# Expert gates of both halves built once in the up stage, the second half's kept in DRAM, and all low parts of the up stage made by GpSimd

## Chip, cores and metric

One core of a Trainium2 chip. The metric is the device time of one launch in microseconds (us), the median of several runs. The profile is one further execution, whose own time stands in the table below.

## The reference, cut to what matters

The program is a transformer block followed by two more layers, for 256 tokens of width 1024 in float32. The part that is changed belongs to the first block's product-key expert layer:

```python
v1, i1 = lax.top_k(s1, 16)                    # per token and head, over 128 keys
v2, i2 = lax.top_k(s2, 16)
cand = (v1[..., :, None] + v2[..., None, :])  # 16 x 16 sums
...
sv, pos = lax.top_k(cand, 16)
eidx = jnp.take_along_axis(i1 * 128 + i2, pos)   # expert number, shortened
gw = softmax(sv)
act = x . u_tab[eidx];  hact = gelu(act) * gw;  y = sum(hact * v_tab[eidx])
```

Each token uses 8 heads x 16 = 128 of 16,384 experts. Expert number = 128 * i1 + i2.

## The kernel before, in words

The kernel does not gather experts. It multiplies all 16,384 rows of `peer_u` with all tokens (the **up stage**), applies gelu, multiplies the result with a dense matrix of gates that is zero for every expert that a token did not choose, and multiplies that with all rows of `peer_v` (the **down stage**). A block is the 128 experts that share one i1. Block b of the activations is a 128 x 256 tile (i2 by tokens), and the 128 blocks lie in two SBUF tensors, `A[0]` for blocks 0 to 63 and `A[1]` for 64 to 127.

Float32 accuracy comes from splitting: every 128 x 1024 weight tile (`wraw`) is copied by ScalarE to a rounded high part (`whi`) and the rest is subtracted into a low part (`wlo`); three matmuls replace one (`mm3`, lines 224 to 229, and `down`, lines 295 to 318). `wraw`, `whi` and `wlo` have three buffers each.

*Up stage* (`u_blocks`, `u_split`, lines 1015 to 1032). For each block: load `peer_u` on SyncE's queue (L249), high part on ScalarE (L1018), low part on GpSimd or VectorE by the set `POOL_U` (L1019), 24 matmuls (L227 to L229), gelu on ScalarE (L1031). Beside it run, by a hand-set ratio of steps per block (`even`): `topk`, blocks 0 to 75, on VectorE; `gates(0)`, blocks 76 to 127; and `ada0`, which loads a 128 x 1024 tile of `ada_w` and reduces it on VectorE (L180), 24 times. While `topk` runs its scratch tiles lie in `A[1]`, which its blocks have not reached.

`gates(half)` (lines 992 to 1009), 32 iterations of 8 tokens: one-hot matrices of i2 (`oa`, L1000) and, for the 64 values of i1 of this half, of i1 (`ob`, L1002) by comparing with `iota`; `ob` times the gate weight (L1003); 8 float32 matmuls give the gates of 8 tokens (L1006; the trace has two instructions for each); VectorE multiplies them into `A[half]` (L1008). The picked indices and weights `iT` lie in SBUF.

*Down stage* (`v_blocks`, lines 1043 to 1052). For each block: load `peer_v` (L249), high part on ScalarE (L1039), low part on VectorE (L1040), the activations split into `wwh` (ScalarE, L217) and `wwl` (VectorE, L222), 12 matmuls of 512 columns (L308, L309, L312). Beside blocks 0 to 63 run `gates(1)` and 40 steps of `ada1` (L180 again), beside blocks 64 to 127 another 32 steps of `ada1`.

Each engine runs its own instructions in order. That order is laid down when the kernel is built, by a scheduler that works on simulated times; program order decides only among what is ready there. So a gate matmul can stand ahead of blocks that come earlier in the program.

Of the kernel before, what the change touches and what calls it, by code (L numbers as in the profile page):

```python
# [18 lines left out]
T = 256  # L19
# [65 lines left out]
def program(tc, I, out, C, taps=None, upto=99):  # L85
# [821 lines left out]
    for c in range(16):  # L907
# [8 lines left out]
        for tt in range(2):  # L916
# [2 lines left out]
    tap("sc", sc)  # L919

    wk = keep.tile([128, 2 * D], F32, name="C8")
    iT = wk[:, 0:768].rearrange("p (j t) -> p j t", j=3)
    iota = wk[:, 768:896]
    oas = itertools.cycle([wk[:, 896:1920].rearrange("p (t i) -> p t i", t=8),
                           wrk.tile([128, 8, 128], F32, name="oa", bufs=1)])
    G.dma_start(iota, C["iota"])

    def topk():
        sels = [flat(b, 1).rearrange("p (s c) -> p s c", s=2) for b in (99, 103)]
        gw = flat(101, 1).rearrange("p (t h k) -> p t h k", t=2, h=8)  # L930
        for tt in range(2):
            rg = flat(88 + 4 * tt, 4)
            v = rg[:, 0:256].rearrange("p (c k) -> p c k", c=16)
            ix = rg[:, 256:512].bitcast(U32).rearrange("p (c k) -> p c k", c=16)
            sv = rg[:, 512:640].rearrange("p (h k) -> p h k", h=8)
            px = rg[:, 640:768].bitcast(U32).rearrange("p (h k) -> p h k", h=8)
            s2 = flat(96, 1)[:, 0:128]
            cand = flat(97, 1)
            for h in range(8):
                for half in range(2):  # L940
                    c = 2 * h + half
                    s1 = sc[:, tt, c]
                    V.max(v[:, c, 0:8], s1)
                    V.max_index(ix[:, c, 0:8], v[:, c, 0:8], s1)
                    V.match_replace(s2, v[:, c, 0:8], s1, -3e38)
                    V.max(v[:, c, 8:16], s2)
                    V.max_index(ix[:, c, 8:16], v[:, c, 8:16], s2)
                yield
                V.tensor_tensor(cand.rearrange("p (a b) -> p a b", a=16),
                                v[:, 2 * h].unsqueeze(2).to_broadcast([128, 16, 16]),  # L950
                                v[:, 2 * h + 1].unsqueeze(1).to_broadcast([128, 16, 16]), op=OP.add)
                V.max(sv[:, h, 0:8], cand)
                V.max_index(px[:, h, 0:8], sv[:, h, 0:8], cand)
                V.match_replace(cand, sv[:, h, 0:8], cand, -3e38)
                V.max(sv[:, h, 8:16], cand)
                V.max_index(px[:, h, 8:16], sv[:, h, 8:16], cand)
                yield

            fx = rg[:, 768:1024].rearrange("p (c k) -> p c k", c=16)
            V.tensor_copy(fx, ix)  # L960
            ab = flat(98, 1).rearrange("p (s h k) -> p s h k", s=2, h=8)
# [19 lines left out]
        V.tensor_reduce(r8, gw, axis=AX.X, op=OP.add)  # L981
        V.reciprocal(r8, r8)
        V.tensor_tensor(gw, gw, r8.unsqueeze(3).to_broadcast([128, 2, 8, 16]), op=OP.mult)
        for tt in range(2):
            pt = ps_tr((128, 384))
            for j, src in enumerate((sels[tt][:, 0], sels[tt][:, 1], gw[:, tt].rearrange("p h k -> p (h k)"))):
                P.transpose(pt[:, j * 128:j * 128 + 128], src, ident)
            ts = slice(tt * 128, tt * 128 + 128)
            V.tensor_copy(iT[:, :, ts], pt.rearrange("p (j t) -> p j t", j=3))
            yield  # L990

    def gates(half):


        io = iota.unsqueeze(1).to_broadcast([128, 8, 128])
        ioh = iota[:, half * 64:half * 64 + 64].unsqueeze(1).to_broadcast([128, 8, 64])
        for t0 in range(0, T, 8):
            ts = slice(t0, t0 + 8)
            oa = next(oas)
            V.tensor_tensor(oa, io, iT[:, 1, ts].unsqueeze(2).to_broadcast([128, 8, 128]), op=OP.is_equal)  # L1000
            ob = wrk.tile([128, 8, 64], F32, name="ob")
            V.tensor_tensor(ob, ioh, iT[:, 0, ts].unsqueeze(2).to_broadcast([128, 8, 64]), op=OP.is_equal)  # L1002
            V.tensor_tensor(ob, ob, iT[:, 2, ts].unsqueeze(2).to_broadcast([128, 8, 64]), op=OP.mult)  # L1003
            pg = ps_tr((128, 8, 64))
            for t in range(8):
                P.matmul(pg[:, t], oa[:, t], ob[:, t], start=True, stop=True)  # L1006
            dst = A[half][:, :, ts]
            V.tensor_tensor(dst, dst, pg.rearrange("p t b -> p b t"), op=OP.mult)  # L1008
            yield

    Ut, Vt = I["peer_u"], I["peer_v"][0]
    POOL_U = set(b for b in range(3, 76) if b % 5) | set(b for b in range(76, 128) if b % 3)
    POOL_V = ()

    def u_split(b):
        raw = unit(Ut[b])
# [19 lines left out]
    def v_split(b):  # L1036
        raw = unit(Vt[b * 128:(b + 1) * 128])
        hi, lo = hilo()
        last_hi[0] = S.activation(hi, raw, AF.Copy)  # L1039
        (G if b in POOL_V else V).tensor_tensor(lo, raw, hi.bitcast(F32), op=OP.subtract)  # L1040
        return hi, lo

    def v_blocks(b0, b1_):
        for b in range(b0, b1_):
            vs = vt.pop(b)
            if b < 126:
                vt[b + 2] = v_split(b + 2)
            wh = wrk.tile([128, T], F32R, name="wwh", bufs=2)
            wl = wrk.tile([128, T], F32R, name="wwl", bufs=2)
# [31 lines left out]
        even(ada0, i, ADA, 100)  # L1081
    for _ in tk:
        pass
    tap("iT", iT)
    g0 = gates(0)
    for i, _ in enumerate(u_blocks(76, 128)):
        even(g0, i, 32, 50)
        even(ada0, i + 76, ADA, 100)
# [628 lines left out]
```

## Time and profile before

| | us |
|---|---|
| median of 3 runs (2226.71 to 2234.04) | 2227.6 |
| the profiled execution, its own time | 2230.72 |
| its span, first to last instruction | 2228.9 |
| TensorE busy, of the span | 2124.5 (95%) |
| VectorE busy | 1697.8 (76%) |
| ScalarE busy | 1011.9 (45%) |
| GpSimd busy | 714.6 (32%) |

A busy time is the sum of an engine's instructions. Matmuls are pipelined, so a TensorE that is busy throughout is not one at its peak; the distance from one matmul's start to the next tells more. In the rows of busy time by stretch the engines stand in the order TensorE matmul (PE), TensorE weight load (PEld), VectorE (DVE), ScalarE (ACT), GpSimd (POOL), each with its count of instructions; the granted TensorE clock, the DMA share and GB/s follow. The up stage runs from about 520 us to 998 us of the span, the first half of the down stage to 1240 us, the second to 1430 us.

### The profile page before, as it was taken

The page shows a single profiled execution, that of the slowest core. Times are in us where ns is not written, and L with a number is a line of the kernel's source. Part 1 is how long each engine was busy: PE and PEld are TensorE (multiplying, and loading weights), DVE is VectorE, ACT ScalarE, POOL GpSimd, SP SyncE. Part 2 cuts the span into 40 slices and gives each one's busy share as a digit, 9 for nine tenths or more (in the row PEclk, how much of TensorE's full clock was granted, in tenths as well). Part 3 has the DMA queues.
Part 4 walks back from the last instruction along what each step waited for, and adds up shares of the span by engine and source line. Part 5 has one row for each costly group of instructions (what it writes and reads, how often), then busy time and mean ns, then how long its engine had stood idle before and what let it go on. Part 6 is the DMA issues. An engine that isn't in the chain of part 4 may idle for free.

```text
span 2228.9 us, 38314 instructions
## 1 busy us (share of the span) xinstructions
PE 2124.5 (95%) x15238; PEld 1966.2 (88%) x15238; DVE 1697.8 (76%) x2671; ACT 1011.9 (45%) x1666; POOL 714.6 (32%) x359
## 2 busy tenths in 40 slices
PE   9999999998788999999999999999989899999999
PEld 8989999998788999998888777899877899888998
DVE  6677688779998456679999787635696778677876
ACT  5645565444343433333443455534533454544554
POOL 2212332203555654430000000132261456344554
PEclk9999999999898999999999999999999999999999
DMA  6544544465454764447667888765331655554552
GB/s 211 162 125 136 166 125 123 152 200 180 166 185 142 227 197 144 130 137 267 234 225 238 295 280 284 195 132 79 71 106 51 231 190 176 180 184 136 187 199 95
DMA packets 108213, 386.84 MB, mean 174 GB/s; under 512 B 13025, under 2 KB 14065, under 8 KB 108034
## 3 DMA queue, kind: packets, MB, share of 16 engines
q1 hardware_dynamic: 106080, 380.04, 52.2%
q0 software_dynamic: 1520, 3.75, 2.7%
q8 instruction: 120, 1.97, 0.4%
q10 hardware_dynamic: 434, 0.59, 0.1%
q14 instruction: 59, 0.48, 0.1%
HBM read 382.18 MB, written 2.16 MB: 172 GB/s over the span
## 4 chain that ended last, share of the span: by engine, by line
PE 66%; DVE 21%; DMA 7%; issue 4%; ACT 2%; SPq 0%; POOL 0%; DVEq 0%; ACTq 0%
PE mm L227 13%; PE mm L228 13%; PE mm L229 13%; PE acc L309 5%; PE acc L312 5%; PE acc L308 4%; PE tr L1006 4%; DMA xdt<-in_ada_w 3%; DVE A L180 2%; DVE wlo L1040 2%; DVE wlo L222 1%; DMA wraw<-in_peer_v 1%; DVE xdt L180 1%; DVE wlox L222 1%; DVE wlo L1019 1%
## 5 line engine op out<-in xcount | busy, mean ns | idle before, releaser
L229 PE MATMUL mm<-xdt,wlo 128*128 128x256 f32 x1248 | 358.9, 288 | 28.7 <-DVE wlo L1019 28.3
L227 PE MATMUL mm<-xdt,whi 128*128 128x256 f32 x1248 | 362.8, 292 | 5.0 <-ACT A L1031 3.6
L1019 POOL TENSOR_TENSOR wlo<-wraw,whi 128x1024 fp32r<-128x1024 f32 x93 | 241.6, 2600 | 282.1 <-ACT whi L1018 278.3
L228 PE MATMUL mm<-xdt,whi 128*128 128x256 f32 x1152 | 331.0, 287 | 0.2 <-DVE xdt L418 0.2
L1018 ACT ACTIVATE whi<-wraw 128x1024 fp32r<-128x1024 f32 x128 | 135.7, 1060 | 299.0 <-PE mm L228 158.9
L229 PEld LDWEIGHTS mm<-xdt,wlo 128*128 128x128 f32 x1248 | 244.8, 196 | 29.9 <-DVE wlo L1019 29.1
L227 PEld LDWEIGHTS mm<-xdt,whi 128*128 128x128 f32 x1248 | 244.2, 196 | 6.5 <-ACT A L1031 4.2
L228 PEld LDWEIGHTS mm<-xdt,whi 128*128 128x128 f32 x1152 | 226.5, 197 | 0.4 <-DVE xdt L418 0.4
L1039 ACT ACTIVATE whi<-wraw 128x1024 fp32r<-128x1024 f32 x128 | 135.9, 1062 | 155.1 <-DMA wraw<-in_peer_v 114.8
L222 POOL TENSOR_TENSOR wlo<-wraw,whi 128x1024 fp32r<-128x1024 f32 x37 | 92.7, 2505 | 308.6 <-ACT whi L217 271.9
L222 DVE TENSOR_TENSOR wlo<-wraw,whi 128x1024 fp32r<-128x1024 f32 x87 | 136.8, 1573 | 50.6 <-ACT whi L217 50.1
L1040 DVE TENSOR_TENSOR wlo<-wraw,whi 128x1024 fp32r<-128x1024 f32 x128 | 155.8, 1218 | 15.8 <-ACT whi L1039 15.8
L227 PE MATMUL mm<-F,whix 128*128 128x256 f32 x560 | 158.6, 284 | 7.1 <-ACT whix L217 4.9
L217 ACT ACTIVATE whi<-wraw 128x1024 fp32r<-128x1024 f32 x124 | 130.8, 1056 | 73.4 <-PE mm L228 41.9
L228 PE MATMUL mm<-F,whix 128*128 128x256 f32 x560 | 158.4, 283 | 0.4 <-DVE F L418 0.4
L229 PE MATMUL mm<-F,wlox 128*128 128x256 f32 x560 | 158.1, 283 | 0.5 <-DVE wlox L222 0.5
L312 PE MATMUL acc<-whi,wwl 128*128 128x512 f32 x512 | 142.9, 400 | 7.1 <-DVE wwl L222 6.8
L308 PE MATMUL acc<-whi,wwh 128*128 128x512 f32 x512 | 145.3, 395 | 0.5 <-ACT wwh L217 0.5
L309 PE MATMUL acc<-wlo,wwh 128*128 128x512 f32 x512 | 144.2, 392 | 0.4 <-DVE wlo L1040 0.3
L275 POOL TENSOR_TENSOR wrawx<-wrawx,grow 128x1024 f32<-128x1024 f32 x38 | 105.8, 2796 | 91.5 <-DMA wrawx<-in_ffn_w_down 65.1
L1360 POOL MEMSET att<- 128x256 f32 x4 | 1.2, 314 | 406.0 <-DVE xdt L180 406.0
L312 PEld LDWEIGHTS acc<-whi,wwl 128*128 128x128 f32 x512 | 92.5, 188 | 31.1 <-DVE wwl L222 13.7
(606 smaller groups left out, 6529.7 us busy)
## 6 DMA issues: line engine op xcount, KB each, us to landing
wraw<-in_peer_u SPq DMA_DIRECT2D x128, 512.0 KB, 3.7
wraw<-in_peer_v SPq DMA_DIRECT2D x128, 512.0 KB, 4.5
xdt<-in_ada_w SPq DMA_DIRECT2D x72, 512.0 KB, 6.3
wraw<-in_ffn_w_up SPq DMA_DIRECT2D x56, 512.0 KB, 4.0
wraw<-in_w_in SPq DMA_DIRECT2D x42, 512.0 KB, 3.9
wrawx<-in_ffn_w_up SPq DMA_DIRECT2D x32, 512.0 KB, 7.1
wrawx<-in_ffn_w_down SPq DMA_DIRECT2D x31, 512.0 KB, 4.9
wrawx<-in_w_in SPq DMA_DIRECT2D x30, 512.0 KB, 3.6
```

The costliest lines, as they stand in the source:

```text
L217: S.activation(hi, raw, AF.Copy)
L222: eng.tensor_tensor(lo, raw, hi.bitcast(F32), op=OP.subtract)
L227: P.matmul(ps, ah, bh, start=start, stop=False)
L228: P.matmul(ps, ah, bl, start=False, stop=False)
L229: P.matmul(ps, al, bh, start=False, stop=stop)
L308: P.matmul(acc[tt][hf], ah, hi[:, fs], start=st_, stop=False, skip_group_check=free)
L309: P.matmul(acc[tt][hf], ah, lo[:, fs], start=False, stop=False, skip_group_check=free)
L312: P.matmul(acc[tt][hf], al, hi[:, fs], start=False, stop=sp_ and not free, skip_group_check=free)
L1018: S.activation(hi, raw, AF.Copy)
L1019: (G if b in POOL_U else V).tensor_tensor(lo, raw, hi.bitcast(F32), op=OP.subtract)
L1039: last_hi[0] = S.activation(hi, raw, AF.Copy)
L1040: (G if b in POOL_V else V).tensor_tensor(lo, raw, hi.bitcast(F32), op=OP.subtract)
```

## The change

1. `gates` runs once, in the up stage, over all 128 values of i1: `ob` grows from 64 to 128 values per token. The half for blocks 0 to 63 is multiplied into `A[0]` at once, in two instructions of 4 tokens; ScalarE copies the other half out of PSUM into a `wwh` or `wwl` tile, and a DMA on ScalarE's queue writes it to DRAM (`gate_scratch`, 64 stores of 128 KB).
2. Beside blocks 0 to 63 of the down stage `late_gates` takes the place of `gates(1)`: 32 loads of 256 KB on SyncE's queue, each into one of two buffers, and one VectorE multiplication each.
3. In `topk` and `gates` one operand of several VectorE instructions with two SBUF inputs is placed in PSUM (`v1`, `fx`, `ab`, the picked indices and weights). Two copies are added for `v1`, and the two rankings of the top-k stand in two loops.
4. `POOL_U` is now every block from 2 on.

```diff
-    iT = wk[:, 0:768].rearrange("p (j t) -> p j t", j=3)
-    iota = wk[:, 768:896]
...
+    iota = wrk.tile([128, 128], F32, name="iota", bufs=1)
...
+        near = ps_acc()
+        v1 = near[:, 0:128].rearrange("p (h k) -> p h k", h=8)
+        fx = near[:, 0:256].rearrange("p (c k) -> p c k", c=16)
+        ab = near[:, 256:512].rearrange("p (s h k) -> p s h k", s=2, h=8)
...
+            V.tensor_copy(v1, v[:, 0::2])
             for h in range(8):
...
-                                v[:, 2 * h].unsqueeze(2).to_broadcast([128, 16, 16]),
+                                v1[:, h].unsqueeze(2).to_broadcast([128, 16, 16]),
...
-            V.tensor_copy(iT[:, :, ts], pt.rearrange("p (j t) -> p j t", j=3))
+            V.tensor_copy(picks[0][:, :, ts], pt[:, 0:256].rearrange("p (j t) -> p j t", j=2))
+            S.activation(picks[1][:, ts], pt[:, 256:384], AF.Copy)
...
+    g1d = nc.dram_tensor("gate_scratch", (32, 128, 2, 256), F32, kind="Internal").ap()
+    ww = itertools.cycle([("wwh", ps_tr), ("wwl", ps_acc)])
...
-    def gates(half):
+    def gates():
+        pick, weight = picks
...
+        for n in range(32):
+            ts = slice(8 * n, 8 * n + 8)
+            oa, ob = next(oas), next(obs)
+            V.tensor_tensor(oa, io, pick[:, 1, ts].unsqueeze(2).to_broadcast([128, 8, 128]), op=OP.is_equal)
+            V.tensor_tensor(ob, io, pick[:, 0, ts].unsqueeze(2).to_broadcast([128, 8, 128]), op=OP.is_equal)
+            V.tensor_tensor(ob, ob, weight[:, ts].unsqueeze(2).to_broadcast([128, 8, 128]), op=OP.mult)
+            for q in range(2):
+                name, pool = next(ww)
+                pg = pool((128, 512)).rearrange("p (t i) -> p t i", t=4)
+                for t in range(4):
+                    P.matmul(pg[:, t], oa[:, 4 * q + t], ob[:, 4 * q + t], start=True, stop=True)
+                dst = A[0][:, :, 8 * n + 4 * q:8 * n + 4 * q + 4]
+                V.tensor_tensor(dst, dst, pg[:, :, 0:64].rearrange("p t b -> p b t"), op=OP.mult)
+                st = ww_tile(name, F32R).bitcast(F32)
+                S.activation(st.rearrange("p (t b) -> p t b", t=4), pg[:, :, 64:128], AF.Copy)
+                S.dma_start(g1d[n, :, q], st)
             yield
+    def late_gates():
+        for n in range(32):
+            g = wrk.tile([128, 8, 128], F32, name=("oa", "ob")[n % 2], bufs=1).rearrange("p t i -> p (t i)")[:, 0:512]
+            Q.dma_start(g, g1d[n].rearrange("p q c -> p (q c)"))
+            dst = A[1][:, :, 8 * n:8 * n + 8]
+            V.tensor_tensor(dst, dst, g.rearrange("p (t b) -> p b t", t=8), op=OP.mult)
+            yield
...
-    POOL_U = set(b for b in range(3, 76) if b % 5) | set(b for b in range(76, 128) if b % 3)
+    POOL_U = range(2, 128)
...
-    g0 = gates(0)
+    g0 = gates()
...
-    g1 = gates(1)
+    g1 = late_gates()
```

## Rows read from the trace of the kernel before

**Rows 1.** Busy time by stretch of the span: its length, each engine's busy us, clock, DMA.

```profile
520.00:706.00 186.00, 148.62 (x1140) 146.41 (x1138) 185.03 (x363) 67.06 (x98) 105.27 (x38) 0.91 0.53 176
706.00:998.00 292.00, 291.88 (x2443) 291.63 (x2444) 180.75 (x185) 106.55 (x162) 136.29 (x55) 0.99 0.52 161
1000.00:1240.00 240.00, 236.48 (x1287) 201.79 (x1285) 234.62 (x345) 94.58 (x128) 0.00 (x0) 1.00 0.73 244
1240.00:1404.00 164.00, 157.02 (x675) 124.05 (x676) 126.02 (x203) 83.49 (x127) 1.26 (x8) 0.99 0.83 283
```

**Rows 2.** Groups by line, 520 to 706 us: busy us, mean ns, idle before.

```profile
L1031 ACT ACTIVATE A<-mm 128x256 f32<-128x256 f32 x47 | 17.3, 367 | 2.2 <-PE mm L229 2.2
L1019 POOL TENSOR_TENSOR wlo<-wraw,whi 128x1024 fp32r<-128x1024 f32 x38 | 105.3, 2776 | 134.5 <-ACT whi L1018 131.5 <-PE mm L229 1.8 <-PE tr L1006 1.1
L1019 DVE TENSOR_TENSOR wlo<-wraw,whi 128x1024 fp32r<-128x1024 f32 x10 | 17.2, 1715 | 0.0
L180 DVE SCALAR_TENSOR_TENSOR A<-A 128x1024 f32<-128x1024 f32 x28 | 57.9, 2076 | 0.8 <-DMA A<-in_ada_w 0.8
L970 DVE TENSOR_TENSOR A<-A,C 128x1024 f32<-128x1024 f32 x8 | 13.9, 1757 | 0.0
L949 DVE TENSOR_TENSOR A<-A 128x256 f32<-128x256 f32 x12 | 11.2, 935 | 0.0
```

**Rows 3.** Waits of TensorE, 520 to 706 us: total us, times, longest.

```profile
PE mm L229 <- DVE wlo L1019: 28.3, 4, 12.4
```

**Rows 4.** Timeline of TensorE: start, us, instruction; from 477, 601, 706, 806 and 1055 us.

```profile
477.17 0.60 PE L917 MATMUL tr<-A,A 128*128 128x128 f32 x4
...
601.42 0.42 PE L227 MATMUL mm<-xdt,whi 128*128 128x256 f32 x1
...
602.06 0.41 PE L227 MATMUL mm<-xdt,whi 128*128 128x256 f32 x1
...
706.12 1.12 PE L1006 MATMUL tr<-ob,oa 128*128 128x64 f32 x4 [5.24 <-DVE C L989]
...
806.63 0.28 PE L227 MATMUL mm<-xdt,whi 128*128 128x256 f32 x1
...
809.51 0.28 PE L227 MATMUL mm<-xdt,whi 128*128 128x256 f32 x1
...
1055.02 1.89 PE L1006 MATMUL tr<-ob,C 128*128 128x64 f32 x16
...
1062.29 1.89 PE L1006 MATMUL tr<-ob,oa 128*128 128x64 f32 x16
```

**Rows 5.** Instructions of single lines, whole run: count, ns min/median/max, first and last start.

```profile
L1000 DVE TENSOR_TENSOR C<-C x32: 1204/1220/3396, 679.8 to 1222.8; 128x1024 f32<-128x1024 f32 x32
...
L1002 DVE TENSOR_TENSOR ob<-C x64: 668/679/2887, 681.0 to 1231.0; 128x512 f32<-128x512 f32 x64
...
L1003 DVE TENSOR_TENSOR ob<-ob,C x64: 673/691/2883, 687.8 to 1235.8; 128x512 f32<-128x512 f32 x64
...
L1008 DVE TENSOR_TENSOR A<-A,tr x64: 667/686/712, 761.2 to 1240.4; 128x512 f32<-128x512 f32 x64
...
L1019 POOL TENSOR_TENSOR wlo<-wraw,whi x93: 2348/2407/4675, 522.0 to 986.6; 128x1024 fp32r<-128x1024 f32 x93
...
L437 ACTq DMA_DIRECT2D out<-scr x2: 350/352/353, 2220.1 to 2225.1; - x2
```

**Rows 6.** Groups by line, 706 to 998 us.

```profile
L1000 DVE TENSOR_TENSOR oa<-C 128x1024 f32<-128x1024 f32 x16 | 34.1, 2132 | 0.3 <-PE tr L1006 0.3
...
L180 DVE SCALAR_TENSOR_TENSOR A<-A 128x1024 f32<-128x1024 f32 x13 | 23.6, 1815 | 22.6 <-DMA A<-in_ada_w 22.6
```

**Rows 7.** Waits of VectorE, 1240 to 1404 us.

```profile
DVE xdt L180 <- DMA xdt<-in_ada_w: 33.4, 24, 3.7
```

**Rows 8.** Busiest 10 us of the down stage for DMA, as in Rows 1.

```profile
1000.00:1010.00 10.00, 10.00 (x51) 8.11 (x50) 4.64 (x5) 3.02 (x5) 0.00 (x0) 1.00 0.94 342
```

**Rows 9.** DMA issues: KB each, median us from issue to landing, 1000 to 1240 us; the last row whole run.

```profile
wraw<-in_peer_v SPq DMA_DIRECT2D x66, 512.0 KB, 6.5
...
out<-scr SPq DMA_DIRECT2D x2, 256.0 KB, 3.7
```

More of the change, by code (lines that the diff above doesn't have):

```diff
@@ L921, in program @@
     wk = keep.tile([128, 2 * D], F32, name="C8")
-    iT = wk[:, 0:768].rearrange("p (j t) -> p j t", j=3)
-    iota = wk[:, 768:896]
-    oas = itertools.cycle([wk[:, 896:1920].rearrange("p (t i) -> p t i", t=8),
-                           wrk.tile([128, 8, 128], F32, name="oa", bufs=1)])
+    oas, obs = (itertools.cycle([wk[:, i * 1024:i * 1024 + 1024].rearrange("p (t i) -> p t i", t=8),
+                                 wrk.tile([128, 8, 128], F32, name=n, bufs=1)]) for i, n in enumerate(("oa", "ob")))
+    iota = wrk.tile([128, 128], F32, name="iota", bufs=1)
     G.dma_start(iota, C["iota"])
+    picks = []
     def topk():
@@ L938, in topk @@
             cand = flat(97, 1)
-            for h in range(8):
[L940 to L948, printed above, removed]
+            for c in range(16):
+                s1 = sc[:, tt, c]
+                V.max(v[:, c, 0:8], s1)
+                V.max_index(ix[:, c, 0:8], v[:, c, 0:8], s1)
+                V.match_replace(s2, v[:, c, 0:8], s1, -3e38)
+                V.max(v[:, c, 8:16], s2)
+                V.max_index(ix[:, c, 8:16], v[:, c, 8:16], s2)
+                if c % 2:
+                    yield
+            V.tensor_copy(v1, v[:, 0::2])
+            for h in range(8):
                 V.tensor_tensor(cand.rearrange("p (a b) -> p a b", a=16),
-                                v[:, 2 * h].unsqueeze(2).to_broadcast([128, 16, 16]),
+                                v1[:, h].unsqueeze(2).to_broadcast([128, 16, 16]),
                                 v[:, 2 * h + 1].unsqueeze(1).to_broadcast([128, 16, 16]), op=OP.add)
@@ L957, in topk @@
                 yield
-            fx = rg[:, 768:1024].rearrange("p (c k) -> p c k", c=16)
             V.tensor_copy(fx, ix)
-            ab = flat(98, 1).rearrange("p (s h k) -> p s h k", s=2, h=8)
             pxi = flat(100, 1).bitcast(U32).rearrange("p (s h k) -> p s h k", s=2, h=8)
@@ L983, in topk @@
         V.tensor_tensor(gw, gw, r8.unsqueeze(3).to_broadcast([128, 2, 8, 16]), op=OP.mult)
+        picks.extend([ps_acc().rearrange("p (j t) -> p j t", j=2), ps_acc((128, T))])
         for tt in range(2):
@@ L988, in topk @@
             ts = slice(tt * 128, tt * 128 + 128)
-            V.tensor_copy(iT[:, :, ts], pt.rearrange("p (j t) -> p j t", j=3))
+            V.tensor_copy(picks[0][:, :, ts], pt[:, 0:256].rearrange("p (j t) -> p j t", j=2))
+            S.activation(picks[1][:, ts], pt[:, 256:384], AF.Copy)
             yield
-    def gates(half):
-        io = iota.unsqueeze(1).to_broadcast([128, 8, 128])
[L996 to L1008, printed above, removed]
@@ new lines, in program, with ww_tile @@
+    g1d = nc.dram_tensor("gate_scratch", (32, 128, 2, 256), F32, kind="Internal").ap()
+    ww = itertools.cycle([("wwh", ps_tr), ("wwl", ps_acc)])
+    def ww_tile(name, dt):
+        return wrk.tile([128, T], dt, name=name, bufs=2)
+    def gates():
+        pick, weight = picks
+        io = iota.unsqueeze(1).to_broadcast([128, 8, 128])
+        for n in range(32):
[14 more added lines that the diff above has]
+                S.dma_start(g1d[n, :, q], st)
+            yield
@@ L1013, in program @@
-    POOL_V = ()
+    POOL_U = range(2, 128)
     def u_split(b):
@@ L1039, in v_split @@
         last_hi[0] = S.activation(hi, raw, AF.Copy)
-        (G if b in POOL_V else V).tensor_tensor(lo, raw, hi.bitcast(F32), op=OP.subtract)
+        V.tensor_tensor(lo, raw, hi.bitcast(F32), op=OP.subtract)
         return hi, lo
@@ L1047, in v_blocks @@
                 vt[b + 2] = v_split(b + 2)
-            wh = wrk.tile([128, T], F32R, name="wwh", bufs=2)
-            wl = wrk.tile([128, T], F32R, name="wwl", bufs=2)
+            wh, wl = ww_tile("wwh", F32R), ww_tile("wwl", F32R)
             split(blk(b), wh, wl)
@@ L1083, in program @@
         pass
-    tap("iT", iT)
-    g0 = gates(0)
+    g0 = gates()
     for i, _ in enumerate(u_blocks(76, 128)):
```

## The prediction

> **What bounds the kernel now.** I read the busy time by stretch first. The up stage falls in two. From 706 to 998 us TensorE is busy throughout; from 520 to 706 us it lacks 37 us and its mean granted clock is 0.91, while VectorE is full (185.0 of 186). In the first half of the down stage TensorE and VectorE are both full (236.5 and 234.6 of 240); in the second neither is, and DMA has its largest share, 0.83 at 283 GB/s [rows 1].
>
> Next, what TensorE's work is worth at full pace, by starts in the timeline. L227 at 806.63 and 809.51 us are 24 matmuls apart: 2.88 us for a block of the up stage. One gate iteration is 16 instructions, 1.9 us; 32 take 61 us. In the down stage two iterations start 7.27 us apart with two blocks between, so a block there is (7.27 - 1.9) / 2 = 2.7 us [rows 4].
>
> So the second part of the up stage, 81 blocks and 32 iterations, is 81 x 2.88 + 61 = 294 us: TensorE's own work fills its 292. The first part passes 47 blocks (47 gelus, [rows 2]), 135 us of work in 186: 50 us are lost there. The waits name the holder: 28.3 us for low parts made by VectorE, where they queue behind the top-k [rows 3], and 5.2 us when TensorE stands before the first gate matmul until L989, the last copy of the top-k, is done at 706 us [rows 4]. The rest is the clock: after it stood, L227 starts at 601.42 and 602.06 us, three matmuls apart, 0.21 us each instead of 0.12, which are the two levels 1.2 and 2.4 GHz [rows 4]. The first half of the down stage is 64 x 2.7 + 61 = 233 us of TensorE's work in 240.
>
> Last, what stretches VectorE. Instructions with two SBUF inputs that normally take 1.2 us take up to 3.4 beside GpSimd (L1000, L1002, L1003), while L1008, with one input in PSUM, never exceeds 0.712 us though 32 of its 64 ran in the same stage [rows 5].
>
> **Part 1, low parts to GpSimd.** 33 low parts leave VectorE, ten of them in the first stretch at 17.2 us [rows 2]. GpSimd takes 2.4 us undisturbed, up to 4.7 [rows 5], against 2.88 us per block. In the first stretch 47 x 2.4 = 113 us, and behind each of some 30 remaining two-input VectorE instructions (28 of L180) it may stand 1.2 us more: 149 us at most, up to 669 us. It does not set the end unless each of its instructions is held so: 47 x 3.6 = 169 us, 689 us.
>
> **Part 2, operands in PSUM.** By [rows 2] L970 is stretched from 8 x 1.2 to 13.9 us, L974's eight alike, L949 from 12 x 0.41 to 11.2: 15 us that go. The two added copies and the moved destinations are under 1 us. L180 keeps both inputs in SBUF and meets a busier GpSimd: its excess of 0.87 us over 1.2 grows with GpSimd's share (105 of 186 us to 113 of about 160, a quarter more): 28 x 0.24 = +7 us. VectorE thus ends the top-k 17 + 15 - 7 = 25 us earlier, at 681 us.
>
> But TensorE's order puts the first gate matmul after 47 blocks, and it can be there at 520 + 135 = 655 us. I take that order as kept; so TensorE stands 26 us before the first gate, and loses 3 us after it at the low clock. This is what is late next. Then 294 us: the up stage ends at 978 instead of 998 us. Bounds: no stall at all, 520 + 430 + 5 = 955 us (a gain of 43); GpSimd as holder, 10 us gained.
>
> **Part 3, gates for both halves.** TensorE pays nothing: L917, float32 with 128 moving columns, starts its four instructions (0.60 - 0.275) / 3 = 0.108 us apart, as the 64-column gates do, (1.89 - 0.27) / 15 = 0.108 [rows 4]. So it is 512 instructions in the up stage as before, and 512 fewer in the down stage, -61 us there. VectorE does per iteration 3 x 1.22 and two multiplications of 256 elements, about 0.4 each (half of L1008's size, 0.34 to 0.69), 4.5 us instead of 1.22 + 0.68 + 0.69 + 0.69 = 3.3 [rows 5]: 143 us and 24 us of L180 [rows 6] lie beside 297 us of TensorE's work. ScalarE gets 64 copies at 0.37 (L1031, same shape) and 64 issues at 0.35 (L437 on its own queue) [rows 2, 5], 46 us more on 107 of 292 [rows 1]: hidden. Without that cover each would delay a high part by 0.7 us. A store has four buffers in rotation, some 18 us; no row has one of 128 KB, the 256 KB one lands in 3.7 us, the 512 KB loads in 6.5 [rows 9]. Two PSUM banks of the picks are released only with the last gates, ahead of the down stage's first matmuls: up to 2 us, put at 2.
>
> **Part 4, the down stage.** 61 us of TensorE's 233 go: 172. VectorE loses 31 x 3.3 = 101 us [rows 5] of 235 and gets 32 x 0.68 for the late multiplications: 155 us. So a third resource decides. 64 loads of 512 KB, 40 of `ada_w` and 32 late ones of 256 KB are 62.9 MB. At the rate of the second half, which has 283 GB/s and no longer a full TensorE, that is 222 us; at the best 10 us, 342 GB/s [rows 8], 184. I take 208, nearer to the rate that was held for 164 us: the second half needs 164 / 56 = 2.93 us a block for a work of 2.7, and VectorE stood 33.4 us there for `ada_w` [rows 7]. Gain 32, bounds 18 and 56. The 32 issues on SyncE's queue (0.35 each) lie ahead of `peer_v` loads; that cost is in those bounds.
>
> The Trainium skill, "DMA: Bandwidth & Descriptors", Specifications, gives some 358 GB/s of HBM for a core. By that figure the 62.9 MB take 176 us, TensorE would stay the bound, and the sum would be some 25 us lower. No stretch here held such a rate; the 342 of 10 us comes nearest.
>
> **Sum.** -20 + 2 - 32 = -50 us on 2230.7, 2181 us; the profiled execution lies 3 us above the median, so **2178**.
>
> **Rivals.**
> - *Everything goes* (0.13): the scheduler puts the first gate later, DMA holds 342 GB/s: -43 - 56, 2129 us. For it: TensorE has nothing else to wait for. Against it: it stood for L989 already.
> - *Given back* (0.20): GpSimd holds the first stretch (10 gained) and DMA runs at 283 GB/s (18): 2200 us. For it: GpSimd's mean of 2.78 us there [rows 2].
> - *The parts don't act* (0.05): the order of the engines turns out such that TensorE waits elsewhere for as long; within 0.3% of 2227.6.
> - *Late loads in step, slower* (0.07): each late load waits for one of two buffers, VectorE stands before its multiplication until it has landed, and the low parts queue behind. Per two blocks 155 / 32 = 4.85 us of work, 1.2 for `ada_w` (33.4 us over 56 blocks, [rows 7]) and the landing of 3.7 [rows 9]: 9.75 us, 312 for the half instead of 240, 2282 us. It decides from 2.0 us of standing per load. Against it: 24 waits of 1.4 us for loads twice as large.
> - *The shared port takes it back, slower* (0.03): the 96 large gate instructions are held by GpSimd in spite of PSUM. With L1000's longest, 3.4 us, 96 x 2.2 = 210 us come to 167, VectorE ends at 681 + 377 = 1058 us, 60 later than now, 2256 us. It decides from (297 - 167) / 96 = 1.35 us each; the mean excess of L1000 now is 0.93 [rows 6], so even that would be hidden.
>
> The Trainium skill, "Perfetto Trace Analysis", Optimizing Scalar/DVE Operations, warns of that last rival: work moved between VectorE and GpSimd may not pay, since they share a read port. The trace agrees for two SBUF inputs and not for L1008.
>
> **How the numbers follow.** The forecast has 0.52, with a range of its own of 2155 to 2198. About 0.3%, 7 us, can be told from no change. Faster: 0.52 + 0.13 + 0.20 = 0.85; same 0.05; slower 0.10. The range 2132 to 2212 holds the forecast and most of the first two rivals, 8 in 10.
>
> **What would show it.** Right: no wait of TensorE for low parts on VectorE, one wait before the first gate of 15 to 30 us, up stage near 458 us; L1000's successors at 1.2 us without long ones; first half of the down stage near 208 us, no gate matmul in it, over 290 GB/s. Wrong: TensorE waiting for GpSimd's low parts in the up stage, or VectorE for late loads over 2 us each in the down stage; gate matmuls of 128 columns more than 0.12 us apart would add to the up stage what they cost.

## The result and the profile after

The changed kernel takes **2163.0 us** (median of 4 runs, 2161.2 to 2166.9) against 2227.2 for the kernel before beside it: a ratio of 0.970, 95% interval 0.9685 to 0.9722. That is 64 us less where 50 were forecast, inside the range. The profiled execution took 2161.2 us, 69.5 less than that of the kernel before; the stages below are read from these two and add up to their difference, not to that of the medians.

Busy time by stretch of the kernel after, with the columns of [rows 1]. The up stage is split at its first gate matmul and ends at 978.8 us (here and below the start of its last gelu), the first half of the down stage (64 blocks) near 1171.

```profile
520.00:689.00 169.00, 144.16 (x1148) 142.36 (x1147) 163.74 (x346) 67.41 (x100) 128.58 (x48) 0.92 0.57 188
689.00:978.00 289.00, 289.00 (x2439) 288.09 (x2438) 163.40 (x187) 129.35 (x226) 191.40 (x79) 1.00 0.62 197
980.00:1110.00 130.00, 119.83 (x503) 93.69 (x502) 124.52 (x175) 56.21 (x81) 0.00 (x0) 0.99 0.95 346
1110.00:1170.00 60.00, 58.85 (x258) 47.47 (x257) 50.22 (x76) 31.23 (x44) 0.00 (x0) 1.00 0.85 305
1170.00:1330.00 160.00, 153.64 (x670) 122.28 (x670) 127.96 (x202) 83.38 (x127) 1.26 (x8) 1.00 0.87 301
```

The up stage has the shape it had: a first stretch in which VectorE is full and TensorE is not, a second one in which TensorE never pauses. It ends 18.9 us earlier (978.8 for 997.7). The first half of the down stage went from 243 to 192 us, with DMA at 346 GB/s where it had 244; the second half is paced as before (2.9 us a block).

TensorE's waits in the kernel after, 520 to 1000 us, answering [rows 3]:

```profile
PE tr L193 <- DVE mods L186: 18.1, 1, 18.1
PE mm L227 <- ACT A L1055: 5.7, 3, 4.3
PE mm L229 <- POOL wlo L1043: 0.6, 3, 0.2
```

TensorE's timeline behind the longest of them, columns of [rows 4]:

```profile
606.36 0.37 PE L193 MATMUL tr<-ident,mods 128*8 128x128 f32 x1 [18.13 <-DVE mods L186]
...
606.74 0.42 PE L228 MATMUL mm<-xdt,whi 128*128 128x256 f32 x1
606.96 0.41 PE L229 MATMUL mm<-xdt,wlo 128*128 128x256 f32 x1
```

No wait for a low part on VectorE is left, and none at the first gate. Instead TensorE stands once, at a transposition of 8 columns by which `ada0` turns its result into a row: VectorE makes that result between steps of the top-k. Behind it matmuls start 0.22 us apart, the lower clock of [rows 4]. The 4.3 us are a gelu behind the softmax exponential, for which ScalarE waits.

Groups by line of the kernel after, 520 to 690 us, answering [rows 2]: L974, L978 and L955 are L970, L974 and L949 of before.

```profile
L180 DVE SCALAR_TENSOR_TENSOR A<-A 128x1024 f32<-128x1024 f32 x28 | 68.0, 2435 | 2.6 <-DMA A<-in_ada_w 2.6
L974 DVE TENSOR_TENSOR A<-acc,iota 128x1024 f32<-128x1024 f32 x8 | 9.7, 1210 | 0.0
...
L955 DVE TENSOR_TENSOR A<-acc,A 128x256 f32<-128x256 f32 x16 | 6.7, 418 | 0.3
```

Single lines of the kernel after, columns of [rows 5]. L994 is the last copy of the top-k, L1012 and L1014 are gate steps, L1019 the gate matmuls, L1023 and L1024 ScalarE's copies and issues.

```profile
L994 DVE COPY acc<-tr x2: 417/425/433, 666.0 to 677.7; 128x256 f32<-128x256 f32 x2
...
L1012 DVE TENSOR_TENSOR C<-iota,acc x16: 1208/1214/1222, 678.2 to 954.3; 128x1024 f32<-128x1024 f32 x16
...
L1014 DVE TENSOR_TENSOR ob<-ob,acc x16: 1197/1222/1222, 686.2 to 961.3; 128x1024 f32<-128x1024 f32 x16
...
L1019 PE MATMUL tr<-C x128: 272/275/275, 689.0 to 964.9; 128*128 128x128 f32 x128
...
L1023 ACT ACTIVATE wwh<-tr x32: 376/384/385, 740.6 to 970.4; 128x256 f32<-128x256 f32 x32
...
L1024 ACTq DMA_DIRECT2D gate_scratch<-wwh x32: 326/326/341, 741.0 to 971.7; - x32
...
L1033 DVE TENSOR_TENSOR A<-A,oa x16: 1078/1087/1111, 980.1 to 1109.2; 128x512 f32<-128x512 f32 x16
```

With one input in PSUM nothing is stretched: the gate steps never exceed 1.222 us beside a GpSimd that is busy 191 of 289 us. L180, with both in SBUF, is stretched more than before (2435 ns on average, 2076 before). The late multiplication L1033 takes 1.09 us, not the 0.68 that the forecast had.

### The profile page after: what moved, and what is told of

The parts are those of the page before. It is cut to its first block, busy times and chain, and to the rows that moved or that the text cites. A ratio compares the mean times of both kernels' runs of the same rounds, so it can differ in the third digit from the quotient of the medians.

```text
span 2159.4 us, 37426 instructions
## 1 busy us (share of the span) xinstructions
PE 2058.1 (95%) x14726; PEld 1898.8 (88%) x14726; DVE 1607.4 (74%) x2576; ACT 1030.4 (48%) x1732; POOL 795.1 (37%) x392
## 4 chain that ended last, share of the span: by engine, by line
PE 68%; DVE 17%; DMA 8%; issue 3%; ACT 3%; POOL 0%; SPq 0%; DVEq 0%; ACTq 0%; POOLq 0%
PE mm L227 15%; PE mm L228 14%; PE mm L229 14%; PE acc L309 4%; PE acc L312 4%; PE acc L308 4%; DMA xdt<-in_ada_w 3%; DMA wraw<-in_peer_v 3%; DVE A L180 3%; DVE wlo L1064 3%; PE tr L1019 1%; PE acc L1019 1%; DVE wlox L222 1%; DVE wlo L222 1%; ACT whi L1063 1%
## 5 line engine op out<-in xcount | busy, mean ns | idle before, releaser
L1043 POOL TENSOR_TENSOR wlo<-wraw,whi 128x1024 fp32r<-128x1024 f32 x126 | 321.3, 2555 | 182.6 <-ACT whi L1042 182.4
L227 PEld LDWEIGHTS mm<-xdt,whi 128*128 128x128 f32 x1248 | 240.5, 193 | 8.6 <-ACT A L1055 6.3
L228 PEld LDWEIGHTS mm<-xdt,whi 128*128 128x128 f32 x1152 | 223.1, 194 | 0.4 <-DVE xdt L418 0.4
L222 POOL TENSOR_TENSOR wlo<-wraw,whi 128x1024 fp32r<-128x1024 f32 x37 | 93.8, 2538 | 308.4 <-ACT whi L217 271.6
L1063 ACT ACTIVATE whi<-wraw 128x1024 fp32r<-128x1024 f32 x128 | 134.6, 1057 | 106.8 <-DMA wraw<-in_peer_v 100.5
L1064 DVE TENSOR_TENSOR wlo<-wraw,whi 128x1024 fp32r<-128x1024 f32 x128 | 155.5, 1220 | 23.1 <-ACT whi L1063 22.9
L222 DVE TENSOR_TENSOR wlo<-wraw,whi 128x1024 fp32r<-128x1024 f32 x87 | 134.9, 1551 | 46.7 <-ACT whi L217 46.3
L217 ACT ACTIVATE whi<-wraw 128x1024 fp32r<-128x1024 f32 x124 | 130.7, 1055 | 71.9 <-PE mm L228 42.4
L309 PE MATMUL acc<-wlo,wwh 128*128 128x512 f32 x512 | 149.9, 395 | 6.6 <-DVE wlo L1064 6.4
L309 PEld LDWEIGHTS acc<-wlo,wwh 128*128 128x128 f32 x512 | 95.5, 189 | 32.3 <-DVE wlo L1064 12.6
```

Source lines behind the costliest of these rows:

```text
L222: eng.tensor_tensor(lo, raw, hi.bitcast(F32), op=OP.subtract)
L227: P.matmul(ps, ah, bh, start=start, stop=False)
L228: P.matmul(ps, ah, bl, start=False, stop=False)
L309: P.matmul(acc[tt][hf], ah, lo[:, fs], start=False, stop=False, skip_group_check=free)
L1043: (G if b in POOL_U else V).tensor_tensor(lo, raw, hi.bitcast(F32), op=OP.subtract)
L1064: V.tensor_tensor(lo, raw, hi.bitcast(F32), op=OP.subtract)
```

## The experiments

Two questions: which parts made the up stage's 19 us, and what the first half of the down stage is bound by. "Median" is of 4 runs (10 for the list alone), the ratio is to the kernel before on the same chip. Gains in us are differences of medians. The kernel before took 2230.4 to 2232.0 us beside the runs from "`ada0` later" on, against 2227.2 beside the changed kernel, so by the ratios those gains are up to 3.5 us larger.

**The list of GpSimd's blocks undone, and alone.**

```diff
-    POOL_U = range(2, 128)
+    POOL_U = set(b for b in range(3, 76) if b % 5) | set(b for b in range(76, 128) if b % 3)
```

> The changed kernel with the old list of blocks whose low parts GpSimd makes. Theory (in the up stage VectorE's lateness in the first stretch, 520 to 690 us, sets what TensorE loses, wherever in its order it meets it): some ten lows of 1.2 to 2 us come back on VectorE in that stretch, so the up stage ends 12 to 20 us later than 978.8 and the whole takes 2175 to 2183 us; TensorE is shown waiting for VectorE's lows again. Rival (GpSimd, less busy, stretches VectorE's two-input steps less, and gives the time back): within 3 us of the changed kernel's 2163.

> The kernel before with only the longer list of GpSimd's blocks (all from the third on); its gates, its operands in SBUF and its down stage stay. Theory: the seventeen us of lows leave VectorE and some of it comes back as longer two-input steps: the up stage ends some 10 us earlier than 997.7, the down stage's first half stays at 244 us, in all about 2217. Rival (GpSimd's lows are the whole of the up stage's gain): 2208. Second rival (the stretching takes all of it back): 2227.

Measured: with the old list 2157.6 us (2155.2 to 2160.1), ratio 0.9692 (0.9663 to 0.972): the intervals overlap with the changed kernel's, the runs do not. The new list alone, on the kernel before: 2235.5 us, ratio 1.003 (1.0015 to 1.0044), slower by 0.3%. **Neither theory nor any of the rivals had that sign.** The up stage ends at 971.4 with the old list (978.8 with the new one) and at 1001.5 with the new list alone (997.7 before). TensorE's waits with the old list, 520 to 1000 us:

```profile
PE mm L229 <- DVE wlo L1043: 13.3, 5, 7.2
PE tr L193 <- DVE mods L186: 3.6, 1, 3.6
```

VectorE's L180 with the old list, groups by line, 520 to 690 us:

```profile
L180 DVE SCALAR_TENSOR_TENSOR A<-A 128x1024 f32<-128x1024 f32 x30 | 63.4, 2121 | 2.5 <-DMA A<-in_ada_w 2.5
```

Its first gate matmuls, single line, 660 to 760 us:

```profile
L1019 PE MATMUL tr<-C x16: 272/274/275, 696.2 to 743.7; 128*128 128x128 f32 x16
```

TensorE's waits with the new list alone, 520 to 1000 us:

```profile
PE tr L193 <- DVE mods L186: 25.7, 1, 25.7
PE tr L987 <- DVE A L976: 9.8, 1, 9.8
PE mm L227 <- ACT A L1031: 6.6, 2, 6.0
```

VectorE does end the top-k earlier with the new list: the first gate comparison starts at 678.2 us instead of 689.6. But the order of the instructions changes too. TensorE comes to its first gate after 47 gelus with the new list and after 52 with the old (41 and 44 without the other parts): five blocks at 2.88 us, 14.4 us of work, moved behind the gate, which comes only 7.2 us sooner (689.0 for 696.2). The difference, 7.2 us, is that of the up stage's ends, 7.4. The waits show the same from their side: they add up to 24.8 us with the new list and 19.2 with the old one, and to 45.2 with the list alone against 37.5 before; the old list's five waits of at most 7.2 us leave the clock of the stretch at 0.97, the single one of 18.1 at 0.92.

**The top-k's operands in SBUF again.**

```diff
-        near = ps_acc()
-        v1 = near[:, 0:128].rearrange("p (h k) -> p h k", h=8)
-        fx = near[:, 0:256].rearrange("p (c k) -> p c k", c=16)
-        ab = near[:, 256:512].rearrange("p (s h k) -> p s h k", s=2, h=8)
+        ab = flat(98, 1).rearrange("p (s h k) -> p s h k", s=2, h=8)
...
+            fx = rg[:, 768:1024].rearrange("p (c k) -> p c k", c=16)
```

> The changed kernel with the three operands of the top-k steps (v1, fx, ab) in SBUF again instead of PSUM. Theory: the steps that read them take about 2 us again instead of 1.2 while GpSimd works, VectorE ends the top-k 15 us later, and the whole takes 2175 to 2183 us. Rival (these steps don't stand on the path of the first stretch): within 3 us of 2163.

Measured: 2179.1 us, ratio 0.9786 (0.9756 to 0.9815); the up stage ends at 996.3, 17.5 us later. Groups by line, 520 to 690 us:

```profile
L971 DVE TENSOR_TENSOR A<-A,iota 128x1024 f32<-128x1024 f32 x8 | 15.7, 1995 | 0.0
L952 DVE TENSOR_TENSOR A<-A 128x256 f32<-128x256 f32 x12 | 15.4, 1280 | 0.0
```

TensorE's longest wait:

```profile
PE tr L193 <- DVE mods L186: 27.5, 1, 27.5
```

Its last copy of the top-k and its first gate matmuls, single lines:

```profile
L991 DVE COPY acc<-tr x2: 421/421/421, 673.1 to 681.6; 128x256 f32<-128x256 f32 x2
...
L1016 PE MATMUL tr<-C x8: 272/275/275, 688.4 to 689.2; 128*128 128x128 f32 x8
```

The prices are the theory's (1995 for 1210 ns, 1280 for 418: 16.6 us for the two groups), and so is the time. Its path is not: VectorE ends the top-k 3.9 us later (681.6 for 677.7) and not 15, and the first gate matmul starts at 688.4 us, no later than in the changed kernel (689.0). What moved is the order again. TensorE comes to that gate after 41 gelus instead of 47, and six blocks at 2.88 us are 17.3 us of work behind the gate instead of ahead of it, with 9.4 us more of standing at the same transposition. So this run shows what the operands in PSUM are worth in all, not that VectorE's shorter steps earn it directly.

**The gate steps reading SBUF.**

```diff
-        pick, weight = picks
+        pick, weight = xh[0][:, 0:2].bitcast(F32), xh[0][:, 2].bitcast(F32)
```

> The changed kernel, its 96 gate steps reading a buffer in SBUF (the high parts of x) in place of the picks and weights in PSUM; this leaves the gates' meaning out, the instructions and their sizes are the same. Theory: each gate step with two inputs in SBUF goes from 1.22 to at most 2.4 us beside GpSimd's lows, VectorE in the second stretch (690 to 978 us) from 163 to at most 252 of 289 us, which is still under TensorE's work: within 5 us of 2163. Rival (the gates' place in the order makes TensorE wait for each): slower by 15 us or more.

Measured: 2193.4 us, ratio 0.9846 (0.9819 to 0.9873); the up stage ends at 1010.4. The longest of the six gate groups, 690 to 1010 us:

```profile
L1013 DVE TENSOR_TENSOR C<-iota,xdt 128x1024 f32<-128x1024 f32 x15 | 42.4, 2824 | 0.0
```

The longest sums in ScalarE's waits for VectorE and in TensorE's waits, 520 to 1010 us:

```profile
ACT wwh L1023 <- DVE A L1021: 84.1, 21, 6.7
...
PE mm L227 <- ACT A L1055: 17.6, 14, 3.9
```

The price per step was right on average: the six groups have 210.3 us in 89 instructions, 2.36 us each (1.87 to 2.82 by group). That it would be hidden was wrong. VectorE is busy 260 of 320 us, so it does not run out of time on average; but a late gate makes ScalarE's copy wait, and the gelu queued behind that copy holds TensorE. The rival had the time right, and its waits in part: TensorE stands 17.6 us for gelus (5.7 in the changed kernel) and some 9 us for gate steps. Its waits add up to 17 us more than in the changed kernel; the up stage is 31.6 us longer, and the rest is open.

**`ada0` later, its rows later, the top-k's transposes later.** Ways to take TensorE's stand away; no instruction is removed.

```diff
-        even(ada0, i, ADA, 100)
+        if i >= 50:
+            even(ada0, i - 50, ADA, 50)
```

> The changed kernel, the 24 steps of ada0 (28 of VectorE's long two-input steps L180 and their transposes) put over blocks 50 to 100 of the up stage, out of the stretch of the top-k. Theory (VectorE's work in the first stretch sets the up stage's loss): TensorE no longer stands 18 us at ada0's row transposes, VectorE ends the top-k earlier, the up stage ends some 25 us earlier, in all about 2138. Rival (the wait moves on, to the first gate or to ada0's loads, which now stand beside the second stretch): a gain under 8 us.

Measured: 2155.9 us (2154.0 to 2157.3), ratio 0.9664 (0.9644 to 0.9684), 7 us less: the rival. TensorE is busy 169.4 of 170 us up to 690. Then it waits, 520 to 972 us:

```profile
PE mm L227 <- ACT A L1055: 8.6, 6, 4.3
PE tr L193 <- DVE mods L186: 6.7, 1, 6.7
```

Here too the order moved. VectorE is busy only 108.2 of the 170 us, yet its last copy of the top-k starts at 720.4 us instead of 677.7 and the first gate matmul at 731.8: with less to do it did not end the top-k earlier, as the theory had it, but later.

```diff
+            with tc.issue_after(last_unit[0].ins):
+                for slot in held_rows:
+                    to_row(slot, mods[:, slot])
```

> The changed kernel, the row transposes of ada0 (where TensorE stood 18.1 us at 588) put behind block 101; the first gate stays behind 47 blocks. Theory (what TensorE loses in the first stretch is set by the place of the first gate in its order against the end of VectorE's top-k, so that a wait removed ahead of it comes back at it): TensorE waits some 20 us at the top-k's transposes or the first gate instead, the up stage ends 0 to 5 us earlier than 978.8. Rival (the 18 us at the rows and the low clock behind them are the loss itself): the up stage ends some 20 us earlier, in all about 2143.

Measured: 2158.2 us, ratio 0.9674 (0.965 to 0.9698); the up stage ends at 976.1. As the theory had it, the wait reappears at the next instruction of the top-k in TensorE's order, one of its transposes:

```profile
PE tr L995 <- DVE A L983: 16.9, 2, 16.5
```

```diff
-                P.transpose(pt[:, j * 128:j * 128 + 128], src, ident)
+                with tc.issue_after(marks[56].ins):
+                    P.transpose(pt[:, j * 128:j * 128 + 128], src, ident)
```

> The changed kernel with ada0's row transposes behind block 101 and the top-k's last six transposes behind block 56 of TensorE's order, so that the first gate comes after 61 blocks instead of 47; no instruction is taken away. Theory (TensorE's order, made for a VectorE that is faster than it is, makes it wait; it has work of its own for the whole time of the top-k): no wait of over 5 us between 520 and 690 us, the up stage ends 20 to 25 us earlier, near 955, in all 2137 to 2143. Rival (the wait moves behind the first gate, since the gates then have a shorter stretch and GpSimd's lows must keep up with TensorE): a gain under 8 us, as with ada0 put late (7.1 us).

Measured: 2163.9 us, ratio 0.9698 (0.9675 to 0.9721): nothing gained, over 20 us off the expectation, and not by the rival's mechanism. ScalarE's timeline shows where the wait went:

```profile
624.13 1.28 ACT L988 ACT_TABLE_LOAD   x1
649.82 0.42 ACT L988 ACTIVATE A<-A 128x256 f32<-128x256 f32 x1 [24.40 <-DVE A L987]
```

Free of its own top-k steps TensorE runs ahead, and now it is ScalarE that comes to the softmax exponential (L988, behind 35 gelus) 24.4 us before VectorE has its input. The gelus queue behind it, and TensorE waits 24.4 us for one. So the wait had to be taken from all engines at once:

```diff
-        S.activation(gw, gw, AF.Exp)
+        with tc.issue_after(gelus[45].ins):
+            S.activation(gw, gw, AF.Exp)
```

> The changed kernel with every step of the top-k's end put later in the order of the engine that carries it: ScalarE's softmax exponential behind the 46th gelu (it came after the 35th in the run with the transposes held, and held the gelus and with them TensorE for 24.4 us), TensorE's last six top-k transposes behind block 54, ada0's row transposes behind block 101; and the second half's gates with the tokens innermost (8.9 us faster by itself). Theory (TensorE loses in the first stretch only because an in-order engine stands before a step of the top-k while VectorE is late, and has work for all that time): no wait of over 5 us between 520 and 700 us, the up stage ends near 953 instead of 978.8, the first half of the down stage is 6 to 8 us shorter, in all 2126 to 2136. Rival (the wait comes back at a third place, the gates or a low part): the up stage ends after 970, in all 2147 to 2156.

Measured: **2138.5 us** (2137.3 to 2143.2), ratio 0.9591 (0.9568 to 0.9615): faster than both kernels, 2.5 us above the expected stretch. The up stage ends at 963.7, so neither near 953, as the theory had it, nor after 970, as the rival had it. TensorE's longest wait group, 520 to 1000 us:

```profile
PE mm L232 <- ACT A L1066: 11.0, 5, 5.6
```

Busy time by stretch, divided near the first gate (705.6 us) and at the ends of the up stage and of the half:

```profile
520.00:700.00 180.00, 167.84 (x1371) 165.70 (x1371) 177.91 (x354) 80.65 (x120) 155.83 (x58) 0.99 0.65 214
700.00:964.00 264.00, 264.00 (x2217) 262.64 (x2216) 151.94 (x181) 134.50 (x207) 167.38 (x69) 1.00 0.61 192
964.00:1151.00 187.00, 177.49 (x759) 139.85 (x758) 163.64 (x251) 87.99 (x126) 0.00 (x0) 1.00 0.93 339
```

Half of the 24.8 us of waits is gone. The rest is again ScalarE, which waits 8.2 us for the last copies of the top-k with gelus behind it.

Over all kernels, the up stage's end (the end of its last gelu) less the sum of TensorE's waits from 520 us on is nearly one number:

| kernel | up stage ends | TensorE's waits | difference |
|---|---|---|---|
| before | 998.0 | 37.5 | 960.5 |
| new list alone | 1001.7 | 45.2 | 956.5 |
| top-k in SBUF | 996.5 | 39.2 | 957.3 |
| transposes held | 980.5 | 28.8 | 951.7 |
| changed kernel | 979.0 | 24.8 | 954.2 |
| rows late | 976.3 | 22.9 | 953.4 |
| old list | 971.6 | 19.2 | 952.4 |
| `ada0` late | 971.6 | 15.7 | 955.9 |
| all held | 963.9 | 12.1 | 951.8 |

It lies around the forecast's bound of 955 for no stall at all: what differs between these kernels is how long TensorE stands, 12 to 45 us. (Gate steps from SBUF are the exception, 1010.6 - 41.7 = 968.9; 8 to 17 us of that stay unexplained.) What spreads the others from 952 to 960 was not followed.

**The first half of the down stage.** Less for VectorE, in two ways; less for DMA, in two ways. TensorE's waits in this half in the changed kernel, 978 to 1165 us; L1063 makes the high parts, L1064 the low parts:

```profile
PE acc L309 <- DVE wlo L1064: 6.2, 8, 1.4
PE acc L308 <- ACT whi L1063: 4.8, 6, 1.0
```

```diff
-            V.tensor_tensor(dst, dst, g.rearrange("p (t b) -> p b t", t=8), op=OP.mult)
+            V.tensor_tensor(dst[:, 0:8], dst[:, 0:8], g.rearrange("p (t b) -> p b t", t=8)[:, 0:8], op=OP.mult)
```

> The changed kernel with the late multiplication done on 8 of its 64 blocks only; seven eighths of it are left out, its loads stay. VectorE has some 28 us less to do in the first half of the down stage, the DMA the same. If the DMA sets this half (346 GB/s): within 3 us of the changed kernel's 2163, and the 65th wwh copy comes within 3 us of 1172. If VectorE sets it (it is busy 124.5 of 130 us): 15 to 20 us faster.

```diff
-                S.activation(st.rearrange("p (t b) -> p t b", t=4), pg[:, :, 64:128], AF.Copy)
+                S.activation(st.rearrange("p (b t) -> p t b", t=4), pg[:, :, 64:128], AF.Copy)
...
-            V.tensor_tensor(dst, dst, g.rearrange("p (t b) -> p b t", t=8), op=OP.mult)
+            dst = dst.rearrange("p b (q t) -> p b q t", q=2)
+            V.tensor_tensor(dst, dst, g.rearrange("p (q b t) -> p b q t", q=2, t=4), op=OP.mult)
```

> The changed kernel, the second half's gates kept in DRAM with the four tokens innermost, so that the late multiplication reads runs of four in place of a full transposition. Its 1087 ns should fall to about 680 to 900, VectorE's work in the first half of the down stage by 6 to 13 us. If VectorE sets that half: 5 to 10 us faster. If the DMA sets it: within 3 us of 2163.

Measured: 2154.1 us for both (2144.0 to 2160.1, and 2148.8 to 2157.3); ratios 0.9648 (0.961 to 0.9685) and 0.9653 (0.9627 to 0.9678). The second meets "if VectorE sets that half"; of the first, neither alternative came out. With the tokens innermost the multiplication takes 685 ns. The half is over near 1161 and 1163 us, from 977.7: 183 and 185 us for 192. Busy time from 980 to 1110 us with the shorter multiplications:

```profile
980.00:1110.00 130.00, 123.32 (x529) 97.70 (x528) 106.64 (x179) 61.26 (x88) 0.00 (x0) 1.00 0.95 358
```

The same with the tokens innermost:

```profile
980.00:1110.00 130.00, 122.61 (x521) 95.77 (x520) 118.31 (x181) 60.56 (x87) 0.00 (x0) 1.00 0.95 358
```

Its multiplication, single line:

```profile
L1034 DVE TENSOR_TENSOR A<-A,oa x16: 684/686/691, 978.9 to 1101.6; 128x512 f32<-128x512 f32 x16
```

TensorE's waits with the tokens innermost, 978 to 1165 us:

```profile
PE acc L308 <- ACT whi L1064: 5.0, 6, 1.0
PE acc L309 <- DVE wlo L1065: 2.2, 4, 0.9
```

Both gain 8.9 us (the half is 9 and 7 us shorter) though one relieves VectorE by 13 us and the other by 26. So VectorE did hold this half, by some 9 us, and behind it stands something else: the wait for high parts is as long as it was, DMA runs at 358 GB/s in both, TensorE is busy 123 of 130.

```diff
+        gs = []
...
-            g = wrk.tile([128, 8, 128], F32, name=("oa", "ob")[n % 2], bufs=1).rearrange("p t i -> p (t i)")[:, 0:512]
-            Q.dma_start(g, g1d[n].rearrange("p q c -> p (q c)"))
+            if n < 2:
+                gs.append(wrk.tile([128, 8, 128], F32, name=("oa", "ob")[n], bufs=1).rearrange("p t i -> p (t i)")[:, 0:512])
+                Q.dma_start(gs[n], g1d[n].rearrange("p q c -> p (q c)"))
+            g = gs[n % 2]
```

> The changed kernel with two late loads in place of 32, their two buffers read by all 32 multiplications; thirty loads (7.9 MB) are left out. If the DMA sets the first half of the down stage: 10 to 23 us faster (7.9 MB at 346 GB/s are 22.7 us). If VectorE sets it: within 3 us of 2163.

Measured: 2177.9 us, ratio 0.9777 (0.9749 to 0.9805): 15 us slower with less to load, so the run does not answer its question. Its multiplication, single line:

```profile
L1036 DVE TENSOR_TENSOR A<-A,oa x16: 1024/1046/1118, 979.6 to 1022.4; 128x512 f32<-128x512 f32 x16
```

Busy time, 990 to 1000 us:

```profile
990.00:1000.00 10.00, 1.76 (x4) 1.47 (x5) 10.00 (x12) 1.06 (x1) 0.00 (x0) 0.50 0.08 14
```

Without loads to pace them all 32 multiplications are done by 1025 us, in front of the low parts, and TensorE stands. The late loads also serve as a clock: they spread VectorE's extra work. The next kernel keeps them, at an eighth of the size.

```diff
+            c = 512 if n < 2 else 64
-            Q.dma_start(g, g1d[n].rearrange("p q c -> p (q c)"))
+            Q.dma_start(g[:, 0:c], g1d[n].rearrange("p q c -> p (q c)")[:, 0:c])
```

> The changed kernel with 30 of the 32 late loads cut to an eighth (6.9 MB less, 20 us at 346 GB/s); each still waits and is waited for where it was, so the 32 multiplications stay spread over the first half of the down stage, which they did not in the run with two loads. They work on stale numbers; the parts of the loads are left out. If the DMA alone sets that half: 10 to 20 us faster. If VectorE alone sets it: within 3 us of 2163. If both stand close to their limits, so that relieving either gives what the other leaves: 5 to 10 us faster, as with the shorter multiplications (8.9 us each).

Measured: 2154.3 us (2151.5 to 2159.3), ratio 0.965 (0.9626 to 0.9674). Busy time of its profiled run, the slowest of the four, whose half ended near 1167 us:

```profile
980.00:1110.00 130.00, 120.81 (x515) 94.89 (x514) 126.97 (x179) 58.92 (x85) 0.00 (x0) 1.00 0.88 300
```

TensorE's waits, 978 to 1165 us; L1067 makes the high parts, L1068 the low parts, L222 VectorE's part of the activations:

```profile
PE acc L309 <- DVE wlo L1068: 4.5, 6, 1.7
PE acc L312 <- DVE wwl L222: 4.2, 9, 1.0
PE acc L308 <- ACT whi L1067: 1.3, 1, 1.3
```

With 6.9 MB less the rate falls to 300 GB/s, VectorE is as full as ever, and the waits change sides: those for high parts, which follow the loads, go from 4.8 to 1.3 us, those for VectorE from 6.2 to 8.7. Shorter multiplications took the waits for VectorE and left those for high parts. The third reading fits: both stand close to their limits. The time alone would not tell it from "DMA alone" (8.7 us by the medians, 11.8 by the ratios), and in this trace the half is only some 4 us shorter. How the gain divides between the two can't be told, as one relieved engine hides what the other leaves.

## Why the prediction was right

**Up stage: the mechanism right, the size right in part by luck, the place and what earned it wrong.** It was to end at 978 us and ended at 978.8. TensorE was to stand 26 us for a VectorE that is late with the top-k; it stood 24.8 us, but at the row transposition and at gelus and not before the first gate. What stands next in an in-order queue decides the place more than the amount: in the rows-late and the transposes-held kernels the place changed and the sum stayed at 22.9 and 28.8.

The luck is in a reading. The gate matmul at 706.12 us [rows 4], which the prediction takes for the first, belongs to the second iteration. The first stood at 692.9 us, behind 44 gelus and not 47:

```profile
L1006 PE MATMUL tr<-ob,C x16: 220/275/275, 692.9 to 694.8; 128*128 128x64 f32 x16
```

With 44 in the prediction's sum TensorE stands 34 us and the up stage ends at 681 + 3 + 84 x 2.88 + 61 = 987 us. 47 was what the changed kernel came to have. Most of its gain of 18.9 us is made up otherwise: the first gate starts 3.9 us sooner (689.0), three more blocks stand ahead of it (8.6 us), and the 5.2 us of standing behind it are gone. VectorE was to end the top-k at 681 instead of 706; its last copy ended at 678.1. But in the kernel before 13.5 us of gate steps stood ahead of that copy (from 679.8 us on), and now none do, which the forecast's 25 us did not count.

The step that failed is "I take that order as kept", and with it the 17 us credited to part 1. Taking the low parts away moved the first gate forward by 3 to 5 blocks (44 to 41, 52 to 47), by more than VectorE gained; the other parts together moved it back by 6 to 8. The two cancelled but for three blocks, and the forecast came out. What moved it from 41 to 47 is the top-k's operands in PSUM, since the kernel without them comes to the first gate after 41 again; the longer gates, which it keeps, are not the cause. By which costs the plan is made no run shows. Part 1 alone costs 3.8 us of the up stage on the kernel before and 7.4 on this one. The gain is that of the other parts: 26.3 us between the kernel before and the one with the old list.

**Part 2** was put at 15 us of VectorE's time; undone, the up stage ends 17.5 us later, by the order more than by VectorE, as said. L180 was to lose 7 us and lost 28 x 0.36 = 10. One reading behind it was loose: only L1000 goes from 1.2 to 3.4 us beside GpSimd; L1002 and L1003, of half the size, go from 0.68 to 2.9 [rows 5].

**Part 3** was priced rightly, copies 0.384 for 0.37, issues 0.326 for 0.35, multiplications 0.42 for 0.4, and hidden, as the full second stretch shows. The 2 us at the hand-over, put down to PSUM banks, are 0.9 us for a high part and 0.9 for a low part. Of the rival with the shared port the mechanism is real: without PSUM a gate step takes 2.36 us, 1.14 more. Its point of decision (1.35 more) was wrong. It was put where VectorE's sum fills the stage; the stage suffers earlier, in part through the copies that ScalarE must make in order.

The Trainium skill, "Perfetto Trace Analysis", Optimizing Scalar/DVE Operations, warns that VectorE and GpSimd share a read port. The trace agrees for steps with two inputs in SBUF (1995 for 1210 ns), and shows no such effect with one of them in PSUM (1.222 us at most).

**Part 4 was mis-sized.** The half was put at 208 us, by a rate between 283 and 342 GB/s nearer to the lower; it took 192, at 346 GB/s for 130 us and 305 after. The 283 of the second half was no limit of the DMA: in the first half, with less for VectorE to do, it moved 358. The bound of -56 for "342 held" was the better estimate (-51). The late multiplication was priced by L1008, which reads PSUM, at 0.68 us and took 1.09, 13 us more on an engine busy 124.5 of 130 us; reading runs of four took these 13 us off again, and 9 off the time. No wait of VectorE for a late load is in the trace, so the rival of 2282 us had no place.

The Trainium skill, "DMA: Bandwidth & Descriptors", Specifications, gives some 358 GB/s per core. The trace agrees over 130 us, with 358 GB/s in two kernels, and not over 10 us, where single stretches lie above 400. By that figure the prediction's 62.9 MB take 176 us: that is 32 us below its 208 and not 25, and just above TensorE's 172.

## What to carry to other kernels

When one engine falls behind and others wait for it in order, a wait that is removed comes back at the next instruction that depends on it, on any engine: sum the waits of the engine that sets the end, and move all dependents together. Work taken from the late engine, or made shorter on it, also moves the order of the others; count in the trace how much of the bounding engine's own work stands before the first dependent. And price an instruction by a row with the same operand places and the same strides.

## What the hardware showed unexpectedly

- A VectorE multiplication of 128x512 that reads one of its two SBUF inputs at a step of 64 elements takes 1087 ns; reading it in runs of four, 685, with GpSimd idle both times.
- One wait of 18.1 us was followed by matmuls 0.22 us apart (the granted clock of the stretch 0.92); with the old list five of up to 7.2 us (13.3 in sum) left that stretch at 0.97.
- The core's DMA held 358 GB/s for 130 us. With 6.9 MB less to move it ran at 300, and the half was only some 4 us shorter in that trace; VectorE was as busy as before (127 of 130 us). That the loads are paced by the engines that free their buffers is the likely reason, not shown by a run of its own.
